# An RWKV-7 layer on one core: the triangular inverse by 16-blocks and matrix products instead of 32-blocks, array halves taken in turn, and a repacked filter product

## The chip, the cores and the metric

The kernel runs on 1 core of one Trainium2 chip. The metric is the device time of one execution in microseconds (us), lower is better. A second number is the span of a profiled execution: the time from its first to its last instruction.

## The reference

The reference is a two-layer sequence model over 1,024 latent tokens and 256 context tokens with a model width of 1,024. Layer 0 has a retention branch and an RWKV-7 branch; layer 1 has a Hyena long convolution and a neighbourhood attention. The change touches two of them. The RWKV scan, for both directions of time (8 heads of 64, state `s` of 64x64 per head):

```python
def rwkv7_scan(r, w, k, v, kk, a, s0):
    def step(s, inp):
        r_t, w_t, k_t, v_t, kk_t, a_t = inp
        sa = jnp.einsum('bhvk,bhk->bhv', s, -kk_t)
        s = s * w_t[:, :, None, :] + sa[..., None] * (kk_t * a_t)[:, :, None, :] + v_t[..., None] * k_t[:, :, None, :]
        return s, jnp.einsum('bhvk,bhk->bhv', s, r_t)
```

and the filters of the long convolution, a small network over positions whose last product is `hid @ w3` (64 rows to 2 orders x 2 directions x 512 channels), times a decaying window.

## The kernel before, in words

A build-time scheduler (`tc`) places all instructions: every engine (PE, the matrix engine; DVE, ACT and POOL, the three that work on vectors; SP, which here only issues transfers) runs its own list in a fixed order and waits where an operand isn't there yet. `high_priority` raises the RWKV code over the rest, so other work fills its gaps.

The RWKV scan (class `Rwkv`) goes over the sequence in 10 groups `g` of 128 tokens, each of two chunks `t` of 64 tokens, for both directions `d`, four pairs `p` of heads and two heads `h` in a pair. `step(k)` issues three things that belong to different groups: the recurrence of group k-2 (`recur`), the merge of group k-1 (`merge`), the preparation of group k (`stage1`).

- `stage1` calls `half` for each direction and half of the heads (`hp`). `half` makes the decay and rate of the tokens by two small products (tile `lora`, L851, 64 rows of the array; the PSUM bank `lo` is single), a tanh on ACT (`tw`, L855) and a chain over DVE, ACT and POOL, whose results are `AR`, `BK` and the transposed `BT`. Then `stage1` multiplies `BK` with `AR` (tile `sc`, L915, 64 rows of the array, the four pairs of one head first and then the four of the other) and masks the product into `Ga` and `Gr` on DVE (L917, L919). It also sets half of each values' tile `UV` to zero on POOL (L925) and loads the other half.
- `inverse`: each chunk needs the inverse of a 64x64 unit triangular matrix for 32 matrices (direction, head, chunk, pair). Their 32x32 diagonal blocks go through memory (`la`) into a layout of one block row per partition (`AL`, one buffer), 31 steps of two DVE operations (L950, L952) do the substitution for all, and the blocks go back through memory (`lt`) into `TT`.
- `merge` joins the two blocks of each matrix with three rounds of 32 products each (`t11p`, `xp`, `t21p`, all L973), each round followed by a copy on ACT and one on DVE (L975).
- `recur` runs over the two chunks: `rp<-SP,AR` (L987), `rp<-UV,Ga` (L990), a copy `RH` (L993), the product with the inverse `up` (L996), a copy into `UV` (L999), the state's update `sp` (L1002, the eight of one head, which write one half of the columns, and then the eight of the other), `S` (L1004, L1005) and `SP` (L1008), and the output `rp<-UV,Gr` (L1010), which ACT copies to `Yg` (L1015) and SP stores to `y` (L1018).

`RwkvOut.block` then normalises finished blocks (tiles `fp`, `fa`, `fv`, ...). Other work that fills this stage on PE is `adaps` (L321) and its small follow-up `adat` (L287), which waits for a DVE copy `adarow` (L284).

The filters (`hyena_kernels`) come at the end of the stage and in the one behind it, between the output products `ops` (L412). For each of 4 channel tiles, 2 orders and 4 quarters, `first` makes four products of 64 rows and 128 columns (`hkps`, L1320), whose left operand takes every eighth position: `hid[r, 2 * q + j::8]`. DVE multiplies them with the window (L1321). A plain fp32 product is shown as two PE records in the trace, a transpose as one.

## Time and profile before

| | us |
|---|---|
| median of 3 runs (2420.06 to 2431.53) | 2421.17 |
| the profiled execution: its time | 2423.35 |
| the profiled execution: its span | 2421.6 |

| engine | busy, us | share of the span |
|---|---|---|
| PE | 2233.8 | 92% |
| DVE | 1212.0 | 50% |
| ACT | 930.4 | 38% |
| POOL | 792.3 | 33% |

The shares are means over stages with different limits. The RWKV stage runs from about 700 to 1291 us (the first `lora` product starts at 696.4 us, the last `Yg` copy at 1290.8 us); the ten inverses lie between 745.4 and 1236 us. The rest of the program is mostly dense products on PE.

### The profile page before, as it was taken

What the parts mean: (1) busy time and instruction counts of PE and PEld (TensorE: products, weight loads), DVE (VectorE), ACT (ScalarE), POOL (GpSimd) and SP (SyncE); (2) the same over time, 40 slices, a digit from 0 to 9 for tenths busy, and PEclk for the clock granted to TensorE, in tenths of its full rate; (3) what the DMA queues carried; (4) which work ended last, traced back from release to release, by engine and by line L of the source; (5) the groups of instructions that cost most, each with busy time, mean ns of one, the idle gap of its engine ahead of it and who ended that gap; (6) DMA issues with size and microseconds to landing.
All of it is one profiled execution on the core that took longest, in us unless ns stands there. A gap on an engine that the chain in (4) does not pass through costs nothing. (4 is left out here: it accounts for less than half of the span.)

```text
span 2421.6 us, 44498 instructions
## 1 busy us (share of the span) xinstructions
PE 2233.8 (92%) x16928; PEld 1880.8 (78%) x16928; DVE 1212.0 (50%) x3075; ACT 930.4 (38%) x1996; POOL 792.3 (33%) x1040
## 2 busy tenths in 40 slices
PE   7999999999989788899788999999989999989997
PEld 3778877777856677677676789889968888878987
DVE  6301222234348688777786645620036666634438
ACT  4321134445345353344335533322124444434432
POOL 2313626453556244333224433521120110010133
PEclk9999999999988687789979899999989999989999
DMA  7323334544276444455545334343166562275453
GB/s 246 94 75 105 118 113 128 151 122 135 91 212 183 113 122 129 108 136 143 132 121 169 118 122 141 118 147 109 57 178 162 148 168 83 65 226 153 133 175 122
DMA packets 398367, 325.16 MB, mean 134 GB/s; under 512 B 135038, under 2 KB 337928, under 8 KB 397898
## 3 DMA queue, kind: packets, MB, share of 16 engines
q1 hardware_dynamic: 398154, 322.32, 46.2%
q8 instruction: 134, 2.20, 0.4%
q14 instruction: 79, 0.65, 0.1%
HBM read 227.06 MB, written 95.17 MB: 133 GB/s over the span
## 5 line engine op out<-in xcount | busy, mean ns | idle before, releaser
L380 POOL TENSOR_TENSOR wlo<-wraw,whi 128x512 fp32r<-128x512 f32 (+1 forms) x60 | 82.5, 1393 | 359.9 <-ACT whi L379 304.9
L412 PE MATMUL dps<-n1hi,whi 128*128 128x512 f32 x448 | 186.7, 417 | 0.1
L412 PE MATMUL dps<-n1hi,wlo 128*128 128x512 f32 x448 | 176.2, 393 | 0.0
L412 PE MATMUL dps<-n1lo,whi 128*128 128x512 f32 x448 | 176.0, 393 | 0.0
L412 PE MATMUL dnp<-wlo,nhi 128*128 128x512 f32 x400 | 159.8, 401 | 2.9 <-POOL wlo L396 2.9
L412 PE MATMUL dnp<-whi,nlo 128*128 128x512 f32 x400 | 158.6, 398 | 0.0
L412 PE MATMUL dnp<-whi,nhi 128*128 128x512 f32 x400 | 154.0, 401 | 1.3 <-ACT whi L395 1.3
L396 POOL TENSOR_TENSOR wlo<-wraw,whi 128x512 fp32r<-128x512 f32 (+1 forms) x72 | 92.3, 1291 | 134.8 <-ACT whi L395 124.9
L412 PE MATMUL mmps<-nhi,whi 128*128 128x512 f32 (+1 forms) x336 | 123.7, 369 | 2.4 <-ACT vto L527 2.3
L321 PE MATMUL adaps<-aw,sc 128*2 128x128 f32 (+1 forms) x640 | 112.9, 333 | 9.9 <-DMA aw<-in_ada_w 9.4
L412 PE MATMUL mmps<-nlo,whi 128*128 128x512 f32 (+1 forms) x336 | 120.9, 362 | 0.0
L412 PE MATMUL mmps<-nhi,wlo 128*128 128x512 f32 (+1 forms) x336 | 119.6, 365 | 0.0
L950 DVE TENSOR_TENSOR tm<-RR,AL 128x126 f32<-128x126 f32 (+22 forms) x310 | 99.7, 322 | 19.3 <-DMA AL<-la 11.9
L1248 POOL TENSOR_TENSOR hn<-hn,xr 128x256 f32<-128x256 f32 x60 | 47.2, 791 | 173.4 <-DVE hn L1247 157.4
L952 DVE TENSOR_TENSOR RR<-RR,tm 128x126 f32<-128x126 f32 (+22 forms) x310 | 97.1, 313 | 6.2
L412 PEld LDWEIGHTS dps<-n1hi,wlo 128*128 128x128 f32 x448 | 84.5, 189 | 18.5
L321 PEld LDWEIGHTS adaps<-aw,sc 128*2 128x2 f32 x640 | 54.9, 94 | 53.7 <-issue 15.2
L412 PE MATMUL ops<-whi,clo 128*128 128x256 f32 x320 | 90.6, 290 | 5.4 <-DVE clo L1181 5.4
L412 PEld LDWEIGHTS dps<-n1hi,whi 128*128 128x128 f32 x448 | 85.5, 191 | 10.9 <-ACT whi L379 0.6
L412 PEld LDWEIGHTS dps<-n1lo,whi 128*128 128x128 f32 x448 | 85.2, 190 | 10.3
L412 PEld LDWEIGHTS dnp<-wlo,nhi 128*128 128x128 f32 x400 | 76.0, 190 | 22.1 <-POOL wlo L396 4.8
L412 PE MATMUL ops<-wlo,chi 128*128 128x256 f32 x320 | 91.7, 288 | 0.0
(400 smaller groups left out, 6235.6 us busy)
## 6 DMA issues: line engine op xcount, KB each, us to landing
aw<-in_ada_w SPq DMA_DIRECT2D x32, 512.0 KB
kkr<-kkr SPq DMA_DIRECT2D x40, 384.0 KB
wraw<-in_odd_w_in SPq DMA_DIRECT2D x56, 256.0 KB
wraw<-in_even_w_in SPq DMA_DIRECT2D x48, 256.0 KB
bi<-in_nab SPq DMA_DIRECT2D x64, 192.0 KB
aw<-in_ada_w SPq DMA_DIRECT2D x8, 1024.0 KB
spec<-KS SPq DMA_DIRECT2D x32, 256.0 KB
h<-hn SPq DMA_DIRECT2D x16, 512.0 KB
```

The source lines that it names most:

```text
L321: nc.tensor.matmul(ps[0:2, :n], self.sc[:, k, :], w[:, k, :], start=k == 0, stop=k == 7)
L380: (lo_eng or nc.gpsimd).tensor_tensor(lo[:, kk:kk + 4], raw, hi[:, kk:kk + 4].bitcast(F32), op=ALU.subtract)
L396: nc.gpsimd.tensor_tensor(lo[:, :n], raw[:, :n], hi[:, :n].bitcast(F32), op=ALU.subtract)
L412: nc.tensor.matmul(ps, a, b, start=start and n == 0, stop=stop and n == 3 * nk - 1)
L950: nc.vector.tensor_tensor(t3, RR[:, 0:n, q:q + 1].to_broadcast([P, n, w]), AL[:, q:q + 1, q + 1:32].to_broadcast([P, n, w]), op=ALU.mult)
L952: nc.vector.tensor_tensor(RR[:, 0:n, q + 1:32], RR[:, 0:n, q + 1:32], t3, op=ALU.add)
L1248: add.tensor_tensor(h[:, cs], h[:, cs], x[:, cs], op=ALU.add)
```

## The change

- **Inverse.** The diagonal blocks are 16x16. The 32 matrices give 128 of them, one for each partition, so one substitution of 15 steps of two DVE operations does all. The blocks D go back to memory in their places inside zeroed 64x64 matrices, plain (`ld`, `dd`) and transposed (`lt`, `dt`; the transpose is a POOL copy). `N` is the part of the matrix off the diagonal blocks, masked on POOL. `merge` first makes H = N x D (j = 0) and then T = D + H x T three times, each of the four rounds in two halves of 16 products of 64x64, which use one PSUM bank (`mg`, one buffer). `AL` has two buffers; `N`, `dd`, `dt` and `HT` have one.
- **Halves in turn.** The `lora` products of both directions, the `sc` products of both heads and the `sp` products of both heads are issued alternately, so that each uses the other half of the array's rows (`lora`, `sc`) or columns (`sp`) than the one before. `lora` and `sc` take two PSUM buffers at once; the pool has three instead of two, and the bank `lo` is gone. `stage1` makes all four halves first and then the `sc` products of both directions.
- **Values' half not cleared.** `rp<-UV,Ga` and `up` use only the 64 rows that they need, so the POOL memset of `UV` falls away.
- **y from ACT.** The stores of `y` are issued by ACT instead of SP.
- **Filters.** The positions are reordered on the host, so that a left operand is 128 neighbouring columns; `w3` gets zero blocks for the other direction, so that one product of 128 rows and 256 columns takes the place of two of 64 rows and 128 columns. DVE multiplies with the window in one operation of 512 elements instead of two of 256.
- `FIN`, the buffers of the normalisation's tiles, goes from 6 to 5.

The removed lines that the printed code above shows are left out here.

```diff
+    w3z = np.zeros((P, 2, 4, 2, P), w3.dtype)
+    for h in range(2):
+        w3z[h * 64:h * 64 + 64, :, :, h] = w3[:, :, h]
+    out["hw3"] = w3z
...
+        Z = pl.tile([P, 1040], F32, name="Z", tag="HT", bufs=1)
+        nc.gpsimd.memset(Z, 0.0)
+        for n in ("ld", "lt"):
+            for j in range(2):
+                nc.sync.dma_start(D[n][j].rearrange("d (a n) -> (d a) n", n=1040), Z)
...
+    def lora(self, g, hp, wa):
+
+        nc, hr = self.s.nc, range(2)
+        pss = [self.b1([P, 2, 2, P], "lora") for _ in hr]
+        for j, w in enumerate((self.w2, self.a2)):
+            for q in range(2):
+                p = 2 * hp + q
+                for d in range(2):
+                    nc.tensor.matmul(pss[d][:, j, q, :], w[HALF[d], p * P:(p + 1) * P], wa[HALF[d], j, :], start=True, stop=True)
+        tws = []
+        for d in range(2):
+            tw = self.pf.tile([P, 2, 2, P], F32, name="tw", tag="tw", bufs=3)
+            for j, b in enumerate((self.hw0, self.ha0)):
+                for q in range(2):
+                    p = 2 * hp + q
+                    dst = tw[:, j, q, :] if d == 0 else tw[:, j, q, ::-1]
+                    nc.scalar.activation(dst, pss[d][:, j, q, :], AF.Tanh, scale=0.5, bias=b[:, 4 * d + p:4 * d + p + 1])
+            tws.append(tw)
+        return tws
+
...
+        for hp in range(2):
+            tws = self.lora(g, hp, wa)
+            for d in range(2):
+                R["ar"][d, hp], bks[d, hp], R["bt"][d, hp] = self.half(g, d, hp, tws[d], PCt)
...
-                for h in range(2):
-                    ps = b1([P, 4, P], "sc")
-                    for p in range(4):
-                        u = (p % 2) * NS + t
-                        nc.tensor.matmul(ps[:, p, :], bks[d, p // 2][HALF[h], u, :], R["ar"][d, p // 2][HALF[h], u, :],
+                pss = [b1([P, 4, P], "sc") for _ in range(2)]
+                for p in range(4):
+                    u = (p % 2) * NS + t
+                    for h in range(2):
+                        nc.tensor.matmul(pss[h][:, p, :], bks[d, p // 2][HALF[h], u, :], R["ar"][d, p // 2][HALF[h], u, :],
                                          start=True, stop=True)
+                for h, ps in enumerate(pss):
...
-                nc.gpsimd.memset(UV[HALF[d]], 0.0)
...
+        s, D, pi, pl = self.s, self.D, self.pi, self.pl
+        nc, C = s.nc, self.C
+        gu = [R["ga"][d].rearrange("p h t q c -> p (h t q) c")[HALF[d]] for d in range(2)]
+        N = R["n"] = pl.tile([P, 16, C], F32, name="N", tag="N", bufs=1)
+        mats = lambda t, d: t[d].rearrange("(u s t) -> s u t", s=65, t=C)[0:C]
+        blocks = lambda t: t.rearrange("d (a n) -> (d a) n", n=1040)[:, :1024].rearrange("a (s t) -> a s t", t=C)[:, :, 0:16]
+        LA, LD, LT = (D[n][g % 2] for n in ("la", "ld", "lt"))
+        for d in range(2):
+            nc.sync.dma_start(mats(LA, d), gu[d])
+        AL = pi.tile([P, 16, 16], F32, name="AL", tag="AL", bufs=2)
+        nc.sync.dma_start(AL, blocks(LA))
+        for d in range(2):
+            nc.gpsimd.tensor_tensor(N[HALF[d]], gu[d], s.k("off")[HALF[d], None, :].to_broadcast([C, 16, C]), op=ALU.mult)
+        RR = pi.tile([P, 16, 16], F32, name="RR", tag="RR", bufs=2)
+        nc.gpsimd.tensor_copy(RR, self.eye)
+        tm = pi.tile([P, 64], F32, name="tm", tag="tm", bufs=2)
+        for q in range(15):
+            n, w = q + 1, 15 - q
             t3 = tm[:, :n * w].rearrange("p (a b) -> p a b", b=w)
...
+                                    AL[:, q:q + 1, q + 1:16].to_broadcast([P, n, w]), op=ALU.mult)
+            nc.vector.tensor_tensor(RR[:, 0:n, q + 1:16], RR[:, 0:n, q + 1:16], t3, op=ALU.add)
+        RT = pi.tile([P, 16, 16], F32, name="RT", tag="RT", bufs=2)
+        nc.gpsimd.tensor_copy(RT, RR.rearrange("p s t -> p t s"))
+        for L, src, n in ((LD, RR, "dd"), (LT, RT, "dt")):
+            nc.sync.dma_start(blocks(L), src)
+            T = R[n] = pl.tile([P, 16, C], F32, name=n, tag=n, bufs=1)
+            for d in range(2):
+                nc.sync.dma_start(T[HALF[d]], mats(L, d))
...
+        nc, pl, C, N, Dd, Dt = self.s.nc, self.pl, self.C, R["n"], R["dd"], R["dt"]
+        HT = pl.tile([P, 16, C], F32, name="HTt", tag="HT", bufs=1)
+        TT = R["tt"] = pl.tile([P, 16, C], F32, name="TT", tag="TT", bufs=2)
+        X = Dd
+        for j in range(4):
+            new = HT if j == 0 else TT
+            for b in (0, 8):
+                ps = self.pc.tile([P, 8, C], F32, name="mg", tag="mg")
+                for u in range(8):
+                    for d in range(2):
+                        lh, rh = (N, Dt) if j == 0 else (HT, X)
+                        nc.tensor.matmul(ps[HALF[d], u, :], lh[HALF[d], b + u, :], rh[HALF[d], b + u, :], start=True, stop=True)
+                bs = slice(b, b + 8)
+                if j == 0:
+                    nc.scalar.copy(new[:, bs], ps)
+                else:
+                    nc.vector.tensor_tensor(new[:, bs], ps, Dd[:, bs], op=ALU.add)
+            if j > 0:
+                X = TT
...
             for h, p, d in each:
-                nc.tensor.matmul(rp[d][HALF[d], p, h, :], R["ga"][d][:, h, t, p, :], uh(d, t, p, h), start=False, stop=True,
+                r = HALF[1 - d]
+                nc.tensor.matmul(rp[d][HALF[d], p, h, :], R["ga"][d][r, h, t, p, :], uh(d, t, p, h)[r], start=False, stop=True,
                                  skip_group_check=True)
...
-                copy[d](RH[HALF[d], d], rp[d][HALF[d]])
+                copy[d](RH[HALF[d]], rp[d][HALF[d]])
...
             for h, p, d in each:
-                nc.tensor.matmul(up[HALF[d], p, h, :], R["tt"][:, (h * 2 + t) * 4 + p, :], RH[:, d, p, h, :], start=True,
+                nc.tensor.matmul(up[HALF[d], p, h, :], R["tt"][HALF[d], (h * 2 + t) * 4 + p, :], RH[HALF[d], p, h, :], start=True,
...
-            for h, p, d in each:
+            for p, d, h in itertools.product(range(4), range(2), range(2)):
...
-                nc.sync.dma_start(o[t if d == 0 else 1 - t], Y[r])
+                nc.scalar.dma_start(o[t if d == 0 else 1 - t], Y[r])
...
+        w3 = pl.tile([P, 2, P], F32, name="hw3", tag="hw3", bufs=2)
+        nc.sync.dma_start(w3, i["hw3"][:, o, ct])
...
+                ps = psp.tile([P, 2, 2, P], F32, name="hkps", tag="mm")
+                for j in range(2):
+                    n2 = 2 * q + j
+                    nc.tensor.matmul(ps[:, j].rearrange("p h c -> p (h c)"), hid[:, n2 * P:n2 * P + P],
+                                     w3.rearrange("p h c -> p (h c)"), start=True, stop=True)
+                nc.vector.tensor_tensor(HK, ps.rearrange("p j h c -> p h j c"), win, op=ALU.mult)
```

The scheduler orders everything anew. Three places show what that does. The first is PE's list at the merge of a group in the middle of the stage: `t11p`, `xp` and `t21p` are its three rounds. Before:

```order
L973 MATMUL t11p<-cst,TT_6116 32x32 x32
L851 MATMUL lora<-wa,w_6096 128x128 x2
L885 MATMUL btp<-cst,BK 128x128 x8
L851 MATMUL lora<-wa,a_6097 128x128 x2
L973 MATMUL xp<-TX,Ga 32x32 x32
L915 MATMUL sc<-AR,BK 128x128 x8
L851 MATMUL lora<-wa,w_6096 128x128 x2
L973 MATMUL t21p<-TT_6116,TY 32x32 x32
L851 MATMUL lora<-wa,a_6097 128x128 x2
L996 MATMUL up<-RH,TT_6116 64x64 x16
```

After (`mg<-dt,N` is round 0, `mg<-dd,HTt` round 1, `mg<-TT,HTt` rounds 2 and 3; x16 is one half of a round, and x32 two halves that follow each other):

```order
L996 MATMUL mg<-dt,N 64x64 x16
L935 MATMUL sc<-AR,BK 128x128 x12
L996 MATMUL mg<-dd,HTt 64x64 x16
L935 MATMUL sc<-AR,BK 128x128 x12
L996 MATMUL mg<-dd,HTt 64x64 x16
L849 MATMUL lora<-wa,w_6097 128x128 x4
L849 MATMUL lora<-wa,a_6098 128x128 x4
L996 MATMUL mg<-TT,HTt 64x64 x32
L1122 MATMUL outT<-cst,fa 128x128 x4
L996 MATMUL mg<-TT,HTt 64x64 x16
L329 MATMUL adaps<-aw,sc 2x128 x5
L903 MATMUL btp<-cst,BK 128x128 x4
```

Three rounds have become eight pieces that need each other, and most have other products between them. Over the whole stage, of the 79 neighbouring pairs of pieces only 4 have nothing in between. The halves of `up` (each one head) and of a `lora` group stand between the last ones.

The second place is DVE's list at the substitution of one group in the middle. Before (a part of its 62 operations):

```order
L950 TENSOR_TENSOR tm<-RR,AL 128x128
L952 TENSOR_TENSOR RR<-RR,tm 128x8x16
L950 TENSOR_TENSOR tm<-RR,AL 128x135
L952 TENSOR_TENSOR RR<-RR,tm 128x9x15
L950 TENSOR_TENSOR tm<-RR,AL 128x126
L999 COPY UV<-up 64x512
L952 TENSOR_TENSOR RR<-RR,tm 128x9x14
L950 TENSOR_TENSOR tm<-RR,AL 128x130
L952 TENSOR_TENSOR RR<-RR,tm 128x10x13
L950 TENSOR_TENSOR tm<-RR,AL 128x120
L919 TENSOR_TENSOR Gr<-sc,cst 128x256 x2
L952 TENSOR_TENSOR RR<-RR,tm 128x10x12
```

After (a part of its 30; a row shows the size of what is written):

```order
L972 TENSOR_TENSOR tm<-RR,AL 128x55
L974 TENSOR_TENSOR RR<-RR,tm 128x5x11
L972 TENSOR_TENSOR tm<-RR,AL 128x60
L974 TENSOR_TENSOR RR<-RR,tm 128x6x10
L972 TENSOR_TENSOR tm<-RR,AL 128x63
L1001 TENSOR_TENSOR TT<-mg,dd 128x512
L974 TENSOR_TENSOR RR<-RR,tm 128x7x9
L972 TENSOR_TENSOR tm<-RR,AL 128x64
L974 TENSOR_TENSOR RR<-RR,tm 128x8x8
L972 TENSOR_TENSOR tm<-RR,AL 128x63
L974 TENSOR_TENSOR RR<-RR,tm 128x9x7
```

The products written are of up to 8x8 elements for each partition where they were of up to 8x17, and there are 15 pairs of them instead of 31.

The third place is SP's list of transfers at the end of a chunk. Before:

```order
L1018 DMA y<-Yg 64x512
L927 DMA UV<-vt 64x512 x2
L1018 DMA y<-Yg 64x512
L940 DMA la<-Ga 32x16x32 x2
L954 DMA lt<-RR 1024x1x32 x2
L943 DMA AL<-la 64x1024
L841 DMA kkr<-kkr 128x6x128 x2
L943 DMA AL<-la 64x1024
L958 DMA TT_6116<-lt 32x16x32 x4
```

After, that is ACT's list at the end of a chunk:

```order
L1028 COPY UV<-up 64x512
L905 ACTIVATE BT<-btp 128x512
L1044 COPY Yg<-rp_11165 64x512
L1047 DMA y<-Yg 64x512
L1044 COPY Yg<-rp_11166 64x512
L905 ACTIVATE BT<-btp 128x512
L1037 COPY SP<-S 64x8x64 x2
L1047 DMA y<-Yg 64x512
```

On SP the stores of `y` stood between the loads of `UV`, `AL` and `kkr` and were issued in their turn; now each stands on ACT behind the copy that fills `Yg`, which ACT makes itself.

## Rows read from the trace of the kernel before

**Rows 1.** Lines of the page's first part: busy time, share of the span and instructions of each engine.

```profile
span 2421.6 us, 44498 instructions
...
PE 2233.8 (92%) x16928; PEld 1880.8 (78%) x16928; DVE 1212.0 (50%) x3075; ACT 930.4 (38%) x1996; POOL 792.3 (33%) x1040
```

**Rows 2.** Busy time of each engine in four stretches of the span: start:end, length, then busy us and instructions of PE, weight loads, DVE, ACT and POOL; the granted clock; the share of time that the transfer engines were busy; GB/s. The first is the stage with the ten inverses, the second its end, the third and the fourth the work behind the scan.

```profile
745.00:1245.00 500.00, 421.63 (x5797) 362.13 (x5796) 395.13 (x1111) 202.45 (x472) 181.08 (x292) 0.82 0.51 129
1201.00:1245.00 44.00, 29.27 (x549) 27.20 (x549) 35.09 (x105) 10.02 (x18) 6.45 (x5) 0.77 0.50 129
1291.00:1440.00 149.00, 139.75 (x755) 113.84 (x753) 86.64 (x200) 69.53 (x134) 69.46 (x72) 0.92 0.43 142
1440.00:1560.00 120.00, 114.54 (x928) 110.37 (x927) 70.40 (x189) 41.91 (x71) 47.21 (x35) 1.00 0.37 119
```

**Rows 3.** Two of PE's groups in the stretch 745 to 1245 us, by line: busy us, mean ns of one, idle time of PE before them and what ended most of it.

```profile
L287 PE MATMUL adat<-cst,adarow 2*128 2x2 f32 x32 | 6.9, 282 | 12.8 <-DVE adarow L284 12.8
L1093 PE MATMUL outT<-cst,fa 128*128 128x128 f32 x16 | 3.1, 323 | 3.5 <-DVE fa L1089 3.5
```

**Rows 4.** Groups of instructions by line over the whole span, of the operations that the change issues in another order or in other number (PE alone): busy us (the time in which at least one was under way), mean ns of one | idle time of PE before them and what ended most of it.

```profile
L915 PE MATMUL sc<-AR,BK 64*128 64x128 f32 x640 | 85.7, 302 | 5.1 <-DVE Gr L919 3.9 <-DVE tm L950 1.0
...
L1002 PE MATMUL sp<-UV,BT 128*64 128x64 f32 x640 | 42.7, 240 | 3.6 <-DVE UV L999 3.6
...
L851 PE MATMUL lora<-wa,w 64*128 64x128 f32 x160 | 34.7, 346 | 1.1 <-ACT tw L855 1.0
...
L851 PE MATMUL lora<-wa,a 64*128 64x128 f32 x160 | 33.6, 339 | 10.1 <-ACT tw L855 10.1
...
L996 PE MATMUL up<-RH,TT 128*64 128x64 f32 x640 | 28.8, 257 | 11.5 <-DVE RH L993 7.8 <-DVE TT L975 3.6
...
L990 PE MATMUL rp<-UV,Ga 128*64 128x64 f32 x640 | 25.5, 228 | 0.0
...
L973 PE MATMUL t21p<-TT,TY 32*32 32x32 f32 x640 | 16.9, 222 | 8.8 <-DVE TY L975 8.7
...
L973 PE MATMUL xp<-TX,Ga 32*32 32x32 f32 x640 | 15.7, 214 | 5.2 <-DVE TX L975 5.2
...
L973 PE MATMUL t11p<-cst,TT 128*32 128x32 f32 x640 | 15.4, 206 | 7.5 <-DMA TT<-lt 7.5
```

**Rows 5.** PE in order of time between 1380 and 1420 us: start us, us, engine, line, operation, tiles, count. The first two rows have products of both row halves, the third has those of one half.

```profile
1386.53 1.94 PE L1320 MATMUL hkps<-hw,hid 64*128 64x128 f32 x8
...
1388.99 1.28 PE L1320 MATMUL hkps<-hw,hid 64*128 64x128 f32 x8
...
1400.48 1.21 PE L1320 MATMUL hkps<-hw,hid 64*128 64x128 f32 x4
```

**Rows 6.** Groups by line over the whole span: the filter products, the product of full height with 256 columns, and the weight loads of the first.

```profile
L1320 PE MATMUL hkps<-hw,hid 64*128 64x128 f32 x256 | 61.2, 434 | 6.3 <-ACT S L1362 2.9 <-DVE HK L1321 2.1 <-DMA hw<-in_hw 0.6
...
L1320 PEld LDWEIGHTS hkps<-hw,hid 64*128 64x128 f32 x256 | 52.4, 326 | 16.1 <-ACT S L1362 4.6 <-issue 3.8 <-DVE HK L1321 3.1
...
L1405 PE MATMUL d1ps<-f,X 128*128 128x256 f32 x128 | 29.6, 379 | 0.0
```

**Rows 7.** Groups by line over the whole span on DVE and POOL: the substitution's two operations, POOL operations of 128x1024 elements, the memset of `UV`, and a DVE operation on 512 elements in PSUM.

```profile
L950 DVE TENSOR_TENSOR tm<-RR,AL 128x126 f32<-128x126 f32 (+22 forms) x310 | 99.7, 322 | 19.3 <-DMA AL<-la 11.9 <-DMA adab<-in_ada_b 1.1
L952 DVE TENSOR_TENSOR RR<-RR,tm 128x126 f32<-128x126 f32 (+22 forms) x310 | 97.1, 313 | 6.2
...
L1191 POOL TENSOR_TENSOR hn<-hn,xr 128x1024 f32<-128x1024 f32 x10 | 32.0, 3201 | 34.2 <-DVE hn L1190 34.2
...
L511 POOL TENSOR_TENSOR T<-U 128x1024 f32<-128x1024 f32 x14 | 26.5, 1891 | 23.1 <-DVE U L508 20.4 <-DVE scm L816 2.7
...
L925 POOL MEMSET UV<- 64x512 f32 x40 | 20.7, 518 | 116.3 <-PE sp L1002 84.9 <-PE rp L1010 28.9 <-ACT BT L887 2.1
...
L1004 DVE TENSOR_TENSOR S<-S,sp 128x512 f32<-128x512 f32 x20 | 13.7, 686 | 13.6 <-PE sp L1002 13.2
```

**Rows 8.** The same for DVE with each shape apart: two of the substitution's smaller shapes.

```profile
L950 DVE TENSOR_TENSOR tm<-RR,AL 128x56 f32<-128x56 f32 x20 | 6.1, 307 | 0.4
...
L952 DVE TENSOR_TENSOR RR<-RR,tm 128x30 f32<-128x30 f32 x20 | 4.6, 228 | 0.5
```

**Rows 9.** One of the three like copies of the merge on DVE (the others are of `xp` and `t21p`), by line L975: count, ns least/median/most, first and last start.

```profile
L975 DVE COPY TX<-t11p x10: 689/689/690, 808.9 to 1247.1; 32x512 f32<-32x512 f32 x10
```

**Rows 10.** Who waited for whom between 740 and 1290 us: us in total, times, longest us.

```profile
DVE tw L876 <- DMA kkr<-kkr: 34.8, 12, 7.5
...
POOL km L878 <- DMA kkr<-kkr: 27.0, 7, 10.3
```

**Rows 11.** The same of SP's own queue.

```profile
SPq L1018 <- ACT Yg L1015: 55.9, 15, 16.5
SPq L881 <- POOL km L880: 40.7, 14, 5.5
SPq L940 <- DVE Gr L919: 37.5, 12, 6.2
```

**Rows 12.** The store of `y`, by its line: count, ns least/median/most, first and last start.

```profile
L1018 SPq DMA_DIRECT2D y<-Yg x40: 446/467/954, 822.1 to 1291.4; - x40
```

**Rows 13.** The page's third part, the queue that carries nearly all transfers: packets, MB, share of 16 engines' span.

```profile
q1 hardware_dynamic: 398154, 322.32, 46.2%
```

96 lines of the change are left out of this document (17 added, 79 removed).

## The prediction

> **What bounds the kernel now.** The page's first part comes first [rows 1]: PE is busy for 92% of the span, DVE for half. The chain that ended last says nothing here, since it covers the tail alone. The stage of the change is read from the table of stretches [rows 2]. From 745 to 1245 us PE is busy for 421.6 of 500 us and its clock is 0.82 of full speed; DVE is busy for 395.1 us, 79%. Behind the scan, from 1291 us on, PE is busy for 94 to 95% at a clock of 0.92 to 1.00. So behind the scan PE's work sets the time, and in the scan PE and DVE hold each other up.
>
> What PE loses in the 500 us has two parts. It stands still for 500 - 421.6 = 78.4 us. And a mean clock of 0.82 between the two levels of 1.2 and 2.4 GHz means the lower one for 36% of the time, 180 us; PE works for 84% of these, 152 us, and does in them what full speed does in half: 76 us lost. I take it that the two go together, since a standing PE is what stands ahead of lower clock here: at the stage's end PE is busy for 29.3 of 44 us, at a clock of 0.77, the lowest of the four stretches [rows 2]. Each us of standing still then costs 76/78.4 = 0.97 us more, a factor of 1.97.
>
> Who ends PE's waits stands in the groups by line [rows 3, 4]. DVE does for `t21p` (8.7 us), `xp` (5.2), `adat` (12.8), `up` (7.8 + 3.6), `sp` (3.6), `sc` (3.9 + 1.0) and `outT` (3.5), together 50.1 us; ACT's `tw` does for `lora`, 1.0 + 10.1 = 11.1 us.
>
> **The change part by part.**
>
> Filters: 256 PE records of 128 columns, 61.2 us, become 128 records of 256 columns at full height. The same number of records of that shape stands in the profile with 29.6 us [rows 6]. That is -31.6 us; the old ones also had weight loads of 326 ns each, which read every eighth position. The work lies between other products in a stretch where PE is busy for 94%, so at least 0.94 of it, 29.6 us, reaches the end.
>
> Halves in turn: the trace has no row of a fp32 product of 64 rows that alternates, but it has columns. `up` and `rp<-UV,Ga`, which alternate between column halves, take 28.8 and 25.5 us for 640 records; `sp`, of the same size, but eight of one half in a row, takes 42.7 us [rows 4]. The ratio is 0.60 to 0.67; I take 0.63. For row halves the nearest rows are the old filter products [rows 5]: eight records with both halves take 1.28 or 1.94 us, four with one half take 1.21 us, and twice that is 2.42. So row halves overlap, by a ratio of 0.53 to 0.80, and 0.63 lies within. `sc` (85.7), `lora` (34.7 + 33.6) and `sp` (42.7) are 196.7 us [rows 4]; 0.37 of it is -73 us.
>
> Merge: 3 rounds of products of 32 columns took 15.4 + 15.7 + 16.9 = 48.0 us [rows 4]. The new one has 10 groups x 4 rounds x 32 products x 2 records = 2,560 records of 64 columns, which alternate; at 25.5 to 28.8 us for 640 that is 102 to 115 us, so +54 to +67, taken as +61. Together, PE's work in the scan changes by -12 us. The ends are -25 (ratio 0.60, cheap merge) and +2 (0.67, dear merge); without any overlap of row halves it is -16 + 61 = +45.
>
> DVE: 620 operations of the substitution, 99.7 + 97.1 = 196.8 us [rows 7], become 300 with a mean of 45 elements (680 elements in 15 steps, where it was 2,856 in 31). Shapes of 30 and 56 elements take 228 and 307 ns [rows 8]; at 0.27 us that is 80 us. Of the merge's copies, 30 on DVE at 0.69 us [rows 9], 21 us, become 60 additions of 512 elements from PSUM at 0.686 us [rows 7], 41 us. DVE loses 97 us of work, and its load falls from 79 to about 60%.
>
> What PE gets of that: the waits of `xp` and `t21p` (13.9 us) go with their rounds. Of the other 36.2 us that DVE ends I take half, since a queue at 60% still makes its callers wait: 18 us. `lora` waited because its single bank was held by the tanh; three buffers take its place, shared with `sc` and `btp`: again half, 5.5 us. That is 37.5 us. Against it stand the merge's 80 pieces, which share one bank, so that each needs the piece before copied out: 0.686 us and a last matmul's 257 ns [rows 4, 7], about 1 us if nothing else is there to do. The program's order has other work in 75 of 79 places; 4 us for the empty ones and 12 us, an estimate, for the thin ones make 16 us, 0.2 us a piece. PE stands still for 21.5 us less; times 1.97 that is -42 us. The ends: nothing given back except `xp` and `t21p`, (16 - 13.9) x 1.97 = +4; all of the 61.2 us given back, (16 - 61.2) x 1.97 = -89.
>
> Costed at nothing: the memset of `UV` goes (20.7 us of POOL, and 116.3 us in which POOL stood at its front [rows 7]). In its place POOL gets 20 masks of `N` (64x1024; rows of 128x1024 take 1.89 and 3.20 us [rows 7], so 38 to 64 us) and two short copies a group; POOL is busy for 181 of 500 us, and that hides them. Behind a mask that waits stand `km`, `AR` and `BK` of the next half, and `btp` on PE waits for those; without the cover each group would pay the two masks, 4 to 6 us. `y` from ACT: 40 issues at 0.467 us [rows 12] are 19 us on an ACT that is busy for 202 of 500 us. SP loses the 55.9 us in which it stood at a `y` store [rows 11]; behind it stood `kkr`, for which DVE and POOL waited 34.8 and 27.0 us [rows 10]. What is late next is the store of `prod` and the write of `la`, at which SP already stands for 40.7 and 37.5 us [rows 11], so I count no gain of its own. Transfers: the pieces of the way through memory rise from some 6,400 to 12,288 a group, half of them of 64 bytes. At the mean of all packets, 0.462 x 16 x 2421.6 us / 398,154 = 45 ns [rows 13], 5,888 more on 16 engines are 17 us a group, and the share of 0.51 [rows 2] becomes 0.84: hidden, but not by much. At the low end they cost nothing. The zeroing of `ld` and `lt` happens once, ahead of the first use. One buffer less for `FIN` meets a side work that isn't on the path; if it were, `outT`'s 3.5 us [rows 3] is the wait that grows.
>
> Sum: -31.6 - 12 - 42 = -86 us on the profiled execution's 2423.35 us: 2337 us. The median of the runs is 2 us lower, so 2335 us.
>
> **Rivals.** (a) PE's own work is the bound and DVE's is hidden anyway: only the work counts, -31.6 - 12 + 4 = -40, 2381 us. For it: PE is busy for 84% of the stage, and the pieces of the order are filled by the scheduler either way. Against it: 50 us of PE's waits that DVE ends.
>
> (b) The two halves of a merge piece do not run together, because they write one bank. Then 2,560 records cost what `sp`'s cost, 171 us, not 108: +62, 2397 us. Against it: `xp` and `t21p` write one bank from two groups of rows and take 15.7 and 16.9 us for 640 records, no more than `t11p`, which uses the full height (15.4) [rows 4]. The Trainium skill has this as a rule (TensorEngine Tiling (Array Packing), Restrictions and Gotchas): different row tiles cannot access the same PSUM bank at the same time; by that rule the time would be 2397 us, and the rows of `xp` show no sign of it. Close to it in time is the case that row halves don't overlap: +57, 2392 us; [rows 5] speak against it.
>
> (c) All that DVE and `tw` hold up is given back: -31.6 - 12 - 89 = -133, 2288 us. For it: load and standing still fall together, and the clock follows. Against it: the recurrence keeps its chain of copies on ACT and DVE.
>
> (d) Slower: the merge's pieces become PE's wait. At 1 us for each of 80 instead of 0.2 PE stands still for 64 us more, times 1.97 is +126: 2461 us. It decides from 86/(80 x 1.97) = 0.55 us above my value, 0.75 us a piece. For it: `t21p` and `xp` already waited 13.9 us in 20 rounds, 0.7 us each, for such a copy [rows 4]. Against it: the 75 filled places, and a DVE with less to do.
>
> (e) No change: gains and new stops cancel, with about 0.75 us a piece: 2410 to 2433 us.
>
> **How the numbers follow.** The likeliest, 2335 (its own range 2300 to 2362), has 0.42. (a) and (b) with its neighbour lie from 2362 to 2409 and have 0.23; (c), from 2268 to 2300, 0.15; (e) 0.08; (d) 0.12. A difference of 0.5%, 12 us, is about what a measurement of this kernel can tell from no change. Faster: 0.42 + 0.23 + 0.15 = 0.80; same 0.08; slower 0.12. The range from 2275 to 2412 leaves out (d), nearly all of (e) and the lowest end of (c), some 0.2.
>
> **What would show it right or wrong.** Filters: their group near 30 us for 128 records. Halves: `sc` near 54, `lora` near 43, `sp` near 27 us. Merge: 102 to 115 us; 171 would be (b). DVE: the substitution near 80 us, and DVE busy for 60% of the stage. PE: waits that DVE ends down to about half, a clock of 0.85 to 0.9 in the stage, and the waits at `mg` near 16 us; 60 us or more there would be (d). The prediction is wrong if `mg` waits for DVE at most pieces, if DVE's waits stay although its work fell, or if SP stands at the small pieces, so that `kkr` and `UV` come late.

## The result, and the profile after

The changed kernel takes 2456.88 us (median of 4 runs, 2449.5 to 2458.31), the kernel before 2426.35 us beside it: a ratio of 1.0108 (95% interval 1.0070 to 1.0147). It is slower by 1.1%, where 3.6% less had been forecast. The profiled execution took 2455.99 us. The lines of it that answer to [rows 1] and [rows 2], the page's first part and the table of stretches:

```profile
span 2454.1 us, 45167 instructions
...
PE 2206.8 (90%) x17440; PEld 1860.0 (76%) x17440; DVE 1155.2 (47%) x2753; ACT 918.0 (37%) x1986; POOL 825.6 (34%) x1038
```

```profile
745.00:1245.00 500.00, 389.60 (x5675) 333.55 (x5676) 318.37 (x759) 187.93 (x463) 215.51 (x297) 0.83 0.61 134
...
1164.00:1310.00 146.00, 97.88 (x1354) 87.74 (x1351) 90.92 (x236) 37.82 (x86) 49.71 (x57) 0.71 0.53 120
```

DVE is busy for 77 us less of the 500 us. Fewer groups of tokens fall into them now, so this flatters the change: over the whole span DVE lost 57 us (1212.0 to 1155.2), where 97 had been forecast. PE now stands still for 110 of the 500 us instead of 78. Over the whole span its work falls by 27.0 us (2233.8 to 2206.8), as much as the filters' group alone loses (61.2 to 34.2), and it stands still 59.5 us longer (187.8 to 247.3): that is the loss. PE's groups over the whole span, to be read against [rows 4] and [rows 6]:

```profile
L935 PE MATMUL sc<-AR,BK 64*128 64x128 f32 x640 | 69.1, 298 | 7.8 <-DVE Gr L940 3.4 <-DVE fry L269 2.7 <-DVE frt L268 1.2
...
L996 PE MATMUL mg<-TT,HTt 64*64 64x64 f32 x1280 | 56.5, 252 | 24.4 <-DVE TT L1001 24.3
...
L1348 PE MATMUL hkps<-hw,hid 128*128 128x256 f32 x128 | 34.2, 390 | 2.6 <-ACT d2r L1404 1.4 <-ACT S L1391 1.1
...
L1025 PE MATMUL up<-RH,TT 64*64 64x64 f32 x640 | 30.1, 245 | 40.4 <-DVE TT L1001 34.9 <-DVE RH L1022 2.7 <-ACT RH L1022 2.5
...
L996 PE MATMUL mg<-dt,N 64*64 64x64 f32 x640 | 29.5, 238 | 13.9 <-DMA dt<-lt 13.9
...
L1031 PE MATMUL sp<-UV,BT 128*64 128x64 f32 x640 | 28.6, 248 | 5.4 <-DVE UV L1028 5.4
...
L996 PE MATMUL mg<-dd,HTt 64*64 64x64 f32 x640 | 24.5, 230 | 3.1 <-DVE TT L1001 2.6 <-ACT HTt L999 0.5
...
L849 PE MATMUL lora<-wa,w 64*128 64x128 f32 x160 | 21.9, 329 | 0.4 <-DVE Gr L940 0.3
...
L849 PE MATMUL lora<-wa,a 64*128 64x128 f32 x160 | 19.5, 302 | 0.0
```

`up`, the first product of the recurrence that needs the inverse, waits 34.9 us for the merge's result `TT`, 3.6 us before. PE is early there and the inverse late. It isn't a busy DVE that holds it: in `a_perdir`, a run below with the first stage in its old order and DVE as busy (317 of the 500 us), the same row waits 0.9 us for `TT`.

```profile
L1014 PE MATMUL up<-RH,TT 64*64 64x64 f32 x640 | 28.7, 240 | 8.2 <-DVE RH L1011 7.2 <-DVE TT L990 0.9
```

Where the lateness comes from is seen in PE's order of time over one group, the fifth (start us, us, engine, line, operation, tiles, count; other work left out):

```profile
906.73 1.48 PE L935 MATMUL sc<-AR,BK 64*128 64x128 f32 x6
...
910.04 1.22 PE L849 MATMUL lora<-wa,w 64*128 64x128 f32 x8
...
924.06 0.66 PE L903 MATMUL btp<-cst,BK 128*128 128x128 f32 x4
...
928.05 0.66 PE L903 MATMUL btp<-cst,BK 128*128 128x128 f32 x4
928.63 0.71 PE L849 MATMUL lora<-wa,w 64*128 64x128 f32 x8
...
944.63 0.65 PE L903 MATMUL btp<-cst,BK 128*128 128x128 f32 x4
...
955.40 0.66 PE L903 MATMUL btp<-cst,BK 128*128 128x128 f32 x4
955.99 0.72 PE L935 MATMUL sc<-AR,BK 64*128 64x128 f32 x8
...
969.93 2.05 PE L935 MATMUL sc<-AR,BK 64*128 64x128 f32 x24
...
973.30 0.71 PE L849 MATMUL lora<-wa,w 64*128 64x128 f32 x8
```

One thing stands behind the other: `lora` of the first halves, their transposes `btp` 14 us later (the chain over ACT, DVE and POOL lies between), then `lora` of the second halves, their transposes, all scores, and only then `lora` of the next group. All of these take their PSUM tiles from one ring of three, in the order in which the code is written, and so a group's first stage is one chain, of 63 us here. The recurrence follows at that pace: the products `sp` of the ten groups start over 544 us (825.3 to 1368.8), before over 469. POOL shows the same from the other side: its work for the halves comes in bursts, and at the mask of `N` it stands until the scores are masked.

```profile
903.00 2.34 POOL L965 TENSOR_TENSOR N<-Ga,cst 64x1024 f32<-64x1024 f32 x1 [18.75 <-DVE Ga L938]
908.82 2.34 POOL L965 TENSOR_TENSOR N<-Ga,cst 64x1024 f32<-64x1024 f32 x1 [3.48 <-DVE Ga L938]
...
966.24 2.35 POOL L965 TENSOR_TENSOR N<-Ga,cst 64x1024 f32<-64x1024 f32 x1 [14.65 <-DVE Ga L938]
973.04 2.35 POOL L965 TENSOR_TENSOR N<-Ga,cst 64x1024 f32<-64x1024 f32 x1 [4.46 <-DVE Ga L938]
```

### The profile page after: what moved, and what is told of

The parts are those of the page before. It is cut to its first block, busy times and chain, and to the rows that moved or that the text cites. A ratio compares the mean times of both kernels' runs of the same rounds, so it can differ in the third digit from the quotient of the medians.

```text
span 2454.1 us, 45167 instructions
## 1 busy us (share of the span) xinstructions
PE 2206.8 (90%) x17440; PEld 1860.0 (76%) x17440; DVE 1155.2 (47%) x2753; ACT 918.0 (37%) x1986; POOL 825.6 (34%) x1038
## 5 line engine op out<-in xcount | busy, mean ns | idle before, releaser
L329 PEld LDWEIGHTS adaps<-aw,sc 128*2 128x2 f32 x640 | 57.0, 96 | 65.6 <-issue 19.5
L965 POOL TENSOR_TENSOR N<-Ga,cst 64x1024 f32<-64x1024 f32 x20 | 47.1, 2354 | 158.3 <-DVE Ga L938 142.9
L420 PEld LDWEIGHTS dps<-n1lo,whi 128*128 128x128 f32 x448 | 85.7, 191 | 10.5
L420 PE MATMUL ops<-whi,chi 128*128 128x256 f32 x320 | 92.3, 291 | 0.0
```

Of the source, the lines that this page charges most:

```text
L329: nc.tensor.matmul(ps[0:2, :n], self.sc[:, k, :], w[:, k, :], start=k == 0, stop=k == 7)
L420: nc.tensor.matmul(ps, a, b, start=start and n == 0, stop=stop and n == 3 * nk - 1)
L965: nc.gpsimd.tensor_tensor(N[HALF[d]], gu[d], s.k("off")[HALF[d], None, :].to_broadcast([C, 16, C]), op=ALU.mult)
```

## The experiments

Theory 1: this chain in the first stage is the loss. Rivals: the masks of `N` on POOL (theory 2), the stops at the merge's pieces (theory 3, the prediction's (d)), and, later, the inverse as a whole, the buffer counts and the side work. Ratios are to the kernel before, run beside them, with their 95% intervals; 0.0100 is 24 us. Runs named `b_` start from the kernel before, those named `a_` from the changed one.

**Filters alone**, `b_filt`: the hunks of `zt`, `w3z` and `first` put into the kernel before.

> The kernel before with the filters' part of the change alone: positions reordered, weights of full height, one product of 256 columns for two of 128. Prediction's term: 29.6 to 31.6 us of PE in a stretch where PE is busy for 94%, so 2426 becomes about 2396, with the products' group near 30 us for 128 records. In the trace of the changed kernel the time from the end of the recurrence to the first dps fell from 268 to 223 us, so the gain could be up to 45 us, 2381. The rival theory, that these products lie beside a chain that sets the end in any case, expects 2420 to 2430.

Measured: 2404.83 us, 0.9878 (0.9846 to 0.9910), some 30 us less by the ratio, 26 by the medians. The term holds within the interval.

**The old first stage**, `a_perdir`:

```diff
+    ps = self.pb.tile([P, 2, 2, P], F32, name="lora", tag="lo", bufs=1)   (in half, as before)
-        for hp in range(2):
-            tws = self.lora(g, hp, wa)
-            for d in range(2): ... self.half(g, d, hp, tws[d], PCt)
         for d in range(2):
+            for hp in range(2): ... self.half(g, d, hp, wa, PCt)
```

The ring for the transposes and scores goes back from three banks to two with it, and `tw` from three buffers to two.

> The changed kernel with the old order of the first stage: for each direction its two halves, then its scores, and lora for one direction at a time in a bank of its own (scores and transposes have two banks, as before). Theory 1: the new order made the first stage of a group one chain (lora, halves, all scores, and only then the next lora), which stretched a group from 50 to 57 us; undoing it gives the period of 50 us or less back, 70 us for ten groups, so 2457 becomes 2370 to 2400 although lora and its alternation are lost. Theory 2: the masks of N, which stand in POOL's order behind the scores, hold the period; they still stand there, so 2440 to 2460. Theory 3, the prediction's rival (d): the stops at the merge's pieces hold it; 2440 to 2460 as well.

Measured: 2435.35 us, 1.0003 (0.9979 to 1.0028): by the ratios 25 us of the loss are gone, less than the 57 to 87 expected.

**The masks on DVE**, `a_ndve`: `nc.gpsimd.tensor_tensor(N[...` becomes `nc.vector.tensor_tensor(N[...`.

> The changed kernel with the two masks of N of a group on VectorE, where the masks of the scores are made, not on GpSimd. Theory 2: GpSimd stood for 142.9 us at these masks between 740 and 1370 us, about 14 us a group, and the next group's work on it stood behind; with the masks gone from its queue the period falls by 4 to 7 us, so 2457 becomes 2390 to 2420. Theory 1: the next group's halves can't go ahead of the scores anyway, since their buffers and lora's bank come free only behind the scores; 2445 to 2460. Theory 3: no change, or 10 us more for the 20 to 40 us that VectorE gets.

Measured: 2450.41 us, 1.0061 (1.0040 to 1.0082). That is 11 us less by the ratios, and the intervals overlap a little. The chain is still there: the scores of the ten groups span 536 us, and 534 in the changed kernel.

**Halves first, but `lora` in a bank of its own**, `a_lo`: the first hunk of `a_perdir` with its ring of two, and for each `hp` the two directions.

> The changed kernel with all four halves first, as changed, but lora for one direction at a time in a bank of its own, as before. It divides theory 1: if lora's place in the ring of banks of the scores makes the chain, the next group's lora and tanh run beside the scores again, and 2457 becomes 2390 to 2420; if the order of halves and scores makes it, the time stays at 2445 to 2470. Theories 2 and 3 expect 2455 to 2470, since lora loses its alternation between row halves.

Measured: 2461.12 us, 1.0105 (1.0063 to 1.0147). The chain is gone although all halves still come first (scores of the ten groups in 474 us), so it is `lora`'s place in the ring that makes it. But the time isn't back, so that the run doesn't divide theory 1 as hoped: the `sc` group takes 90.6 us here, and 70.4 in `a_perdir`, and the output blocks end late, as is shown with `a_ahead` below.

**Alternation of `sc` and `sp` alone on top of the filters**, `b_alt`, **and with the memset of `UV` away, 64-row products and `y` from ACT**, `b_cheap` (hunks of the change):

> The kernel before with the filters' part and the alternation of the score and state products (sc and sp) alone; the old inverse, the old lora and everything else stay. In the changed kernel these two groups take 69.1 and 28.6 us instead of 85.7 and 42.7, 31 us less of PE's work. The prediction's step (PE's work counts in full, and the clock with it) expects 2405 to become 2365 to 2380. If PE's work in the scan lies beside a chain of waits, the freed time turns into standing still: 2390 to 2405.

> The run above (filters, sc and sp alternating) and, beside it, what the prediction costed at nothing: the memset of UV goes (products of Ga and TT over 64 rows), y is stored from ScalarE. The old inverse stays. The prediction expects the time of the run above within 5 us. The rival, that the 116 us in which GpSimd stood at the memset and the 56 us in which SP stood at y were worth something, expects 10 to 25 us less. What lies between this run and the changed kernel with the first stage undone (2435) is then the price of the new inverse with its merge.

Measured: `b_alt` 2413.56 us, 0.9935 (0.9912 to 0.9958); `b_cheap` 2395.73 us, 0.9858 (0.9819 to 0.9897). Alternation alone gives nothing here and probably costs; together with the edits costed at nothing it comes out some 5 us below the filters alone, which the intervals don't tell from nothing.

**Scores right behind their own halves, `lora` still in the ring**, `a_early`, **and `lora` of the next group ahead of the last scores**, `a_ahead`:

```diff
-            tw = ... tag="tw", bufs=3   (in lora)
+            tw = ... tag="tw", bufs=4   (in lora)
-        for hp in range(2):
-            tws = self.lora(g, hp, wa)
-            for d in range(2): ... self.half(g, d, hp, tws[d], PCt)
+        tws = [self.lora(g, hp, wa) for hp in range(2)]
         for d in range(2):
+            for hp in range(2): ... self.half(g, d, hp, tws[hp][d], PCt)
+            if d == 1 and g + 1 < self.NG:          (a_ahead alone)
+                self.tws = self.loras(g + 1)
```

> The changed kernel with the scores of the first direction right behind its own two halves; lora of all four halves stays in front, alternating, in the ring of three banks that it shares with transposes and scores. If the order of halves and scores made the loss, 2457 becomes 2400 to 2430. If lora's place in the ring made it (the next group's lora gets a bank only behind the last scores), the group's period stays at 55 to 58 us and the time at 2440 to 2460.

> The run above, and lora of the next group is written ahead of the last scores of this one, so that in the ring it comes before them; banks and buffers are the same. If lora's place in the ring made the loss, the period falls to 50 us or less, the recurrence ends near 1300 us instead of 1369, PE's standing still up to the first dps falls from 161 us to about 100 to 125 us, and 2457 becomes 2385 to 2420. If the chain of the inverse (scores, way through memory, substitution, second way, merge, up) sets the period, it stays at 2440 to 2460.

Measured: `a_early` 2428.66 us, 0.9980 (0.9961 to 0.9998), 28 us less than the changed kernel (31 by the ratios) for the order and the fourth buffer of `tw` that it needs. `a_ahead` 2449.62 us, 1.0068 (1.0048 to 1.0088), though its recurrence ends at 1283 us instead of 1369. The scan got its 86 us back and the kernel 7 of them (18 between the two traced executions, 2455.99 and 2437.80 us). The transposes of the output blocks behind the scan, first and last start us of them:

```profile
L1127 PE MATMUL outT<-cst,fa x32: 272/273/475, 1262.7 to 1439.5; 128*128 128x128 f32 x32
its engine sat idle before it (us, times) until:
  DVE fa L1123: 21.1, 5
```

The blocks come one behind the other, start late, and PE stands for 21 us at them. What follows them on PE are the output products `ops`, here with first and last start in the changed kernel, `a_perdir`, `a_lo` and `a_ahead`:

```profile
L420 PE MATMUL ops<-whi,chi x320: 274/282/682, 1427.8 to 1591.4; 128*128 128x256 f32 x160
L420 PE MATMUL ops<-whi,chi x320: 274/281/562, 1413.2 to 1555.3; 128*128 128x256 f32 x160
L420 PE MATMUL ops<-whi,chi x320: 274/281/562, 1436.4 to 1578.1; 128*128 128x256 f32 x160
L420 PE MATMUL ops<-whi,chi x320: 274/281/561, 1439.5 to 1579.0; 128*128 128x256 f32 x160
```

In the traces of all runs they start at most 2.3 us behind the last transpose of the blocks, the next layer's first product (`dps`) at most 2 us behind the last of them, and from there to the end it is 856 to 866 us whatever was changed. So what an edit does to the time shows in two places: when the last block comes, and how long the `ops` take, with the filter work that is left between them. In the changed kernel the last block comes at 1425.6 us, and the filters go on to 1478.8 us; `ops` take 164 us. In `a_lo` and `a_ahead` the scan ends some 80 us earlier and the filters are through by 1407 us, so `ops` take 142 and 140 us, about the least in any run; but the last block comes at 1436.3 and 1439.5 us, and PE stands for 50 and 52 us between the scan's end and the next layer, 15 in the changed kernel. So the scan's end alone doesn't set the time.

**Six buffers for the output blocks**, `a_perdir_f6` (`FIN = 6`), **two of the merge's four rounds left out**, `a_merge2` (`for j in range(2)`; both on `a_perdir`), **half of the old substitution left out**, `b_half` (`for q in range(0, 31, 2)` on `b_cheap`; like `a_merge2` it doesn't compute the reference), and **`b_cheap` without alternation**, `b_k64y`:

> The run with the old order of the first stage (2435), with six buffers for the output blocks behind the scan instead of five. In the runs whose recurrence ends early PE stands for 13 us at one transpose of the last output block and the first dps comes late, though the scan is over by 1300 us. If the missing buffer makes that, 2435 becomes 2410 to 2422; the prediction costed it at nothing, 2430 to 2440.

> The same run (old order of the first stage, five buffers) with the last two of the merge's four rounds left out, so that the inverse is cut short and the result is not the reference's. It takes away 1,280 products, 55 us of PE's work, 40 pieces and 40 additions on VectorE. If the merge's work and pieces are what the new inverse costs, 2435 becomes 2360 to 2390; if the chain of the group (scores, memory, substitution, memory) sets the time, 2415 to 2435.

> The kernel before with the filters' part, alternation, no memset and y from ScalarE (2396), and of the old substitution every second step left out, so that the inverse and the result are not the reference's. VectorE loses some 98 us of work, as in the change, and nothing is put in its place. The prediction's step (VectorE's relief gives PE 37.5 us of its waits back, times 1.97 with the clock) expects 2396 to become 2315 to 2335; all of its waits given back, 2290. If PE's waits do not follow VectorE's load, 2375 to 2395.

> The kernel before with the filters' part, no memset of UV (products of Ga and TT over 64 rows) and y stored from ScalarE, but scores and state products in the old order of halves. Alternation alone gave nothing (2405 became 2414), so that without it the 2396 of the run with both should become 2383 to 2392; if the alternation pays once GpSimd and SP are free of these waits, 2400 to 2415. It is the candidate for a version faster than both kernels.

Measured: `a_perdir_f6` 2429.87 us, 0.9993 (0.9967 to 1.0019), no difference. `a_merge2` 2415.25 us, 0.9940 (0.9920 to 0.9961): half of the merge, 40 pieces with 55 us of PE, is worth 15 us by the ratios (20 by the medians), 0.4 us a piece with all their work. `b_k64y` 2427.16 us, 0.9982 (0.9964 to 1.0000): 31 us above `b_cheap`; the expectation was wrong. `b_half` 2380.92 us, 0.9801 (0.9776 to 0.9826): 91 us of the substitution away (DVE's busy time as a whole falls by 65), 14 us of time. Its trace and that of `b_cheap` show where the rest went. `b_cheap` (the stretch of 500 us; the state products, the transposes of the output blocks and the first products of the next layer with first and last start):

```profile
745.00:1245.00 500.00, 411.99 (x5954) 351.57 (x5953) 399.58 (x1131) 208.84 (x492) 163.03 (x252) 0.80 0.52 132
```

```profile
L1009 PE MATMUL sp<-UV,BT x640: 222/222/369, 817.8 to 1277.5; 128*64 128x64 f32 x160
...
L1100 PE MATMUL outT<-cst,fa x32: 272/273/474, 1186.6 to 1378.5; 128*128 128x128 f32 x32
...
L418 PE MATMUL dps<-n1hi,whi x87: 389/389/774, 1528.0 to 1599.7; 128*128 128x512 f32 x87
```

and `b_half`:

```profile
745.00:1245.00 500.00, 430.14 (x6383) 365.54 (x6381) 349.71 (x847) 234.73 (x547) 179.07 (x275) 0.87 0.55 142
```

```profile
L1009 PE MATMUL sp<-UV,BT x640: 222/222/369, 811.3 to 1223.9; 128*64 128x64 f32 x160
...
L1100 PE MATMUL outT<-cst,fa x32: 272/273/445, 1200.4 to 1374.4; 128*128 128x128 f32 x32
...
L418 PE MATMUL dps<-n1hi,whi x102: 387/389/495, 1516.9 to 1599.9; 128*128 128x512 f32 x102
```

The scan does gain: PE stands for 18 us less of the 500, the clock rises from 0.80 to 0.87, and the recurrence ends 53.6 us earlier. But the output blocks end only 4 us earlier and the next layer starts 11 us earlier.

**Buffer counts** (`kkr` and `tw` 3 instead of 2, `FIN` 5, as in the changed kernel; on `b_cheap`), `b_bufs`, **the new first stage on top of them**, `b_stage1`, **and a higher priority for the output blocks** (on `b_cheap`), `b_prio`:

> The run with the filters' part, alternation, no memset and y from ScalarE and the old inverse (2396), with the buffer counts of the changed kernel (three for kkr and tw, five for the output blocks instead of two, two and six). The counts cost nothing by the prediction: 2390 to 2402, and then the 34 us up to the run with the new inverse are the inverse's. If the counts (or the order into which the scheduler then puts the work) make the difference, 2415 to 2430.

> The run above with the first stage of the changed kernel: all four halves ahead of all scores, lora of both directions alternating in the ring of three banks. The old inverse stays. If the new order costs by itself, it is 20 to 35 us slower than the run above, and the recurrence ends 40 to 80 us later; if it only costs with the masks of N on GpSimd behind the scores, it is as fast as the run above or, since lora's alternation takes 26 us of PE's work away, 10 to 25 us faster.

> The 2396 run with a higher priority for the output blocks of the scan in the scheduler's order; in the order that it makes the last modulation product and the first of the last eight output blocks then stand some 170 of PE's rows earlier, ahead of the last scores instead of behind them. In the runs the last output block ended 143 to 165 us before the first dps whatever the scan did. If that row of side work sets the end, 2396 becomes 2375 to 2390; if the scan and PE's work set it, 2392 to 2402.

Measured: `b_bufs` 2418.09 us, 0.9946 (0.9918 to 0.9975). `b_stage1` 2466.54 us, 1.0148 (1.0098 to 1.0198): the new first stage costs 49 us with the old inverse too, so the masks of `N` aren't needed for it. `b_prio` 2414.03 us, 0.9939 (0.9921 to 0.9957), slower than `b_cheap`; its scan got longer in the new order (recurrence to 1309 us instead of 1278), so that it says nothing on the blocks.

**Side work given out later**, `a_back` (`SD = (4,4,6,6,8,8,10,10,12,12,8)`), **and seven buffers for the output blocks**, `b_fin7` (on `b_cheap`):

> The changed kernel with its side work given out later: per step 4, 4, 6, 6, 8, 8, 10, 10, 12 and 12 pieces instead of 8 each; the last modulation products then stand behind the last scores in PE's order. If the lonely stretch of 146 us (a third of it standing still, at a clock of 0.71) is what the new order costs, 2457 becomes 2425 to 2440. If the scan's own chain is the cost wherever the side work lies, the early part becomes emptier by as much as the late one fills, and the time stays at 2450 to 2465.

> The 2396 run with seven buffers for the output blocks instead of six; PE's order stays the same but for a few rows at the end. If the blocks behind the scan, 23 to 25 us each, are held by buffers, 2396 becomes 2375 to 2388; if they are one chain of their own or the filters' row sets the end, 2390 to 2402.

Measured: `a_back` 2457.48 us, 1.0097 (1.0061 to 1.0133); `b_fin7` 2403.48 us, 0.9879 (0.9850 to 0.9908), no gain. In `a_back` the stretch in which the scan had been alone is filled:

```profile
1164.00:1310.00 146.00, 115.99 (x1716) 100.01 (x1713) 84.80 (x221) 45.59 (x102) 40.69 (x44) 0.84 0.55 135
```

PE is busy there for 116 us instead of 98 and the clock is 0.84 instead of 0.71, and the time is the same: the idea that the empty late stretch is the loss falls. The recurrence ends at 1362 us, in the changed kernel at 1369: the chain is nearly as long wherever the side work lies.

**The order again, with the old inverse**, `b_early`: the edit of `a_early` on `b_stage1`, with the fourth buffer of `tw`.

> The run with the old inverse and the new first stage (2467), with the scores of a direction right behind its own two halves; lora stays alternating in the ring, in front of both directions. With the new inverse the same edit took 28 us (2457 to 2429). If the order of halves and scores is the cost whatever inverse follows, 2467 becomes 2420 to 2440 and the period of a group falls from 57 to about 52 us; if lora in the ring is the cost, 2455 to 2470.

Measured: 2419.42 us, 0.9944 (0.9922 to 0.9966), 50 us less than `b_stage1`. The scores of the ten groups, first and last start, in `b_stage1`

```profile
L932 PE MATMUL sc<-AR,BK x640: 271/272/579, 724.7 to 1246.7; 64*128 64x128 f32 x160
```

and in `b_early`

```profile
L931 PE MATMUL sc<-AR,BK x640: 272/272/579, 716.0 to 1194.4; 64*128 64x128 f32 x160
```

span 522 and 478 us. The same number is 534 us in the changed kernel, 518 in `a_back`, 536 in `a_ndve`, and 478 in the kernel before, 479 in `a_perdir`, 487 in `a_early`. In `b_bufs`, `b_prio` and `b_k64y`, which have the old first stage, it is 492, 498 and 501 us: the runs with the changed kernel's first stage stand above all others, though not far above the last of these.

## Why the prediction was wrong, step by step

The runs make a staircase; each row has the edits of the rows above.

| added | run | ratio (95% interval) | step, us |
|---|---|---|---|
| filters | `b_filt` | 0.9878 (0.9846 to 0.9910) | -30 |
| `sc`, `sp` in turn, no memset, `y` from ACT | `b_cheap` | 0.9858 (0.9819 to 0.9897) | -5 |
| buffer counts | `b_bufs` | 0.9946 (0.9918 to 0.9975) | +21 |
| `lora` in turn, in the ring, ahead of all halves | `b_early` | 0.9944 (0.9922 to 0.9966) | 0 |
| new inverse and merge | `a_early` | 0.9980 (0.9961 to 0.9998) | +9 |
| all halves ahead of all scores, second `lora` between | the change | 1.0108 (1.0070 to 1.0147) | +31 |

The steps are differences of ratios times 2430 us; one of 9 us is at the edge of what the intervals can tell, and one of 5 below it. One thing goes back on the way: `tw` has four buffers in `b_early` and `a_early`, three in the change.

The sum of the prediction was -86 us: -44 of work, -21.5 of standing still, and the clock. Measured, PE's work falls by 27 us and its standing still grows by 59.5.

- **Filters, -31.6 us: right.** -30 us by the ratios. The group takes 34.2 us, 27.0 less than before, so the work was costed some 5 us too high.
- **PE's work in the scan, -12 us: mis-sized.** `lora` takes 34.7 us as a tile (43 forecast; its two rows, 21.9 and 19.5 us, overlap), `sp` 28.6 (27), the merge 56.5 + 29.5 + 24.5 = 110.5 (102 to 115). `sc` takes 69.1, not 54: its ratio is 0.81, not 0.63. So the work changed by 62.5 - 16.6 - 33.6 - 14.1 = -2 us, which fits PE's 27.0 us less in all, the filters' own. By the prediction's way of adding that is 10 us of the error of 122. `lora` as a tile, before and after (the stretch, its length, PE busy with `lora`, records, then clock and transfers of the whole stretch):

```profile
690.00:1560.00 870.00, 68.35 (x320) 0.87 0.49 136
690.00:1560.00 870.00, 34.73 (x320) 0.87 0.56 140
```

- **"Halves in turn ... -73 us" as time: not borne out.** In `b_alt` `sc` and `sp` fell from 130.9 to 107.9 us against `b_filt`, and the time didn't fall but rose by some 14 us. Against `b_k64y`, with the memset gone and `y` on ACT, the same alternation is worth 30 us (`b_cheap`). So no run shows that a us of this work is a us of time, and why the two pairs differ is open.
- **"That is 37.5 us ... times 1.97", the waits given back: the step that failed most.** Forecast was 21.5 us less of standing still; PE stood still 59.5 us longer over the span. The step has two faults. First, it took PE's waits for DVE as a matter of DVE's load. In `b_half` 91 us less of the substitution on DVE gave 18 us of standing in the stage, and 14 us of time: the scan ended 54 us earlier and the output blocks and the next layer did not follow. Second, it took the ring of three banks for a gain: "three buffers take its place, shared with `sc` and `btp`: again half, 5.5 us". The text on the change says that all four halves come ahead of the scores, and no term of the sum priced it. `lora`'s own waits did go, from 11.2 to 0.4 us; the price shows elsewhere, at `up`. In that order the ring puts the second `lora` behind the first halves' transposes and the next group's behind the last scores (`a_early` undoes the first of the two, and moves half of the scores forward and gives `tw` a fourth buffer with it). The step costs 31 us with the new inverse and 49 with the old. The Trainium skill (Perfetto Trace Analysis, Matmuls) has independent groups of products rotate through different banks so that copying one out overlaps the next group's products. They rotate here, and the trace shows the other side: products that depend on each other's chains, in one ring, wait in the order in which they are written.
- **The factor 1.97 for the clock: wrong.** PE stood for 78 us of the 500 at a clock of 0.82 before, for 110 at 0.83 after, 88 at 0.80 in `b_cheap` and 70 at 0.87 in `b_half`. Over the whole span it was 0.939 before and 0.940 after. A sum of standing still doesn't give the clock.
- **DVE's terms: right in kind.** The substitution takes 48.2 + 45.3 = 93.5 us (80 forecast), the additions 41.0 (41), the load is 64% (60):

```profile
L972 DVE TENSOR_TENSOR tm<-RR,AL 128x15 f32<-128x15 f32 (+4 forms) x150 | 48.2, 321 | 22.5 <-DMA AL<-la 19.2
...
L974 DVE TENSOR_TENSOR RR<-RR,tm 128x15 f32<-128x15 f32 (+4 forms) x150 | 45.3, 302 | 3.8
...
L1001 DVE TENSOR_TENSOR TT<-mg,dd 128x512 f32<-128x512 f32 x60 | 41.0, 684 | 11.4 <-PE mg L996 10.8
```

- **Costed at nothing.** The masks of `N` took 47.1 us of POOL (38 to 64 forecast), and POOL stood 142.9 us at them, but moving them to DVE gave 11 us by ratios whose intervals overlap. SP stood 117.5 us for the masks of the scores at the write of `la`, where it had been 37.5 [rows 11]; that is the chain again. The transfers are right in number: 58,962 packets more, 5,896 a group (5,888 forecast), at a share of 0.61, not 0.84. `FIN` alone is nothing (`a_perdir_f6`, `b_fin7`). The buffer counts together, of which the prediction names only `FIN`, cost 21 us, and no row says which of them and how: this stays open. So does why the edits to `UV` and `y` cost 25 us without alternation (`b_k64y` against `b_filt`) and give 19 with it (`b_cheap` against `b_alt`). The scheduler orders everything anew with each edit, and that alone seems to move the time by some 20 us; that is argued, not shown.
- **The rivals.** 2457 us lies 4 us from rival (d), and it isn't (d): the merge's products wait 41 us, 27 of them for DVE, more than the 16 that the sum had but below the 60 that (d) asked for, and half of the pieces are worth 15 us. `up`'s 34.9 us are for the merge's last piece too; but in `a_perdir` the pieces wait 40 us as well, `up` 0.9, and the time is that of the kernel before. (b) is refuted by the merge's 110.5 us. "DVE's waits stay although its work fell" is what came true, at `up`.
- **What stays open beside these:** `a_lo` and `a_ahead` lose the chain and little of the time. Their traces show where it goes: the last output block comes at 1436 and 1440 us, and the `ops` stand behind it. Why their last eight blocks start as late as 1253 and 1263 us (1202 in the changed kernel, 1229 in `a_perdir`) no run has tested, nor the dearer `sc` of `a_lo`. So the price of the order is measured three times (`a_perdir`, `a_early`, `b_early`: 25, 31 and 50 us), and that the chain in the ring is the whole of it isn't shown.

`b_cheap`, the change without its new first stage, inverse and buffer counts, beats both kernels: 2395.73 us, 1.4% below the kernel before; the filters alone, at 1.2%, can't be told from it.

## What to carry to other kernels

Before counting what a relieved engine gives back, follow one group through the stage and ask which product takes which buffer behind which other one: a bank shared by steps of one chain turns their written order into a wait. A stage that ends earlier is worth only what the next one can start earlier, so look there for the row that starts it. And where a scheduler sets the order, price each part by a run of its own, on top of the others and alone, before the parts are added up.

## What the runs showed of the hardware that was not expected

- Products of 64 rows in turn gain unequally: `lora` falls from 68.3 to 34.7 us, `sc`, of the same shape, from 85.7 to 69.1 us. The mean of one stays near 300 ns; what changes is how many are under way at once (for `sc` 640 x 298 ns in 69.1 us, 2.8 on the mean, where it was 2.3). And the gain of `sc` isn't steady: in the runs in which it alternates the group takes 69.1 to 90.6 us, in the three in which it doesn't 82.9 to 86.5.
- The merge's products, of both row halves into one PSUM bank, take 110.5 us for 2,560 records, 43 ns each, as `up` (47 ns) and `rp<-UV,Ga` (24.8 us for 640, 39 ns).
- More standing still went with no lower clock (78 us at 0.82, 110 at 0.83).
